# Mixing stage of a decoder trunk: transposes by 64 rows into two banks, v centred on quarters, weighted values by halves of the queries, v turned one tile later

## The chip, the cores and the metric

The kernel runs on one core of a Trainium2 chip. The core has a matrix engine (TensorE, PE in the profile), a vector engine (VectorE, DVE), an engine for activation functions and copies (ScalarE, ACT), a general one (GpSimd, POOL) and a queue engine for loads (SyncE, SP). They work side by side and wait for each other by semaphores; each runs its own instructions in order. TensorE reads from the on-chip memory SBUF and writes only to PSUM, eight banks of 128 partitions by 512 fp32 values; ScalarE or VectorE carry results from there back to SBUF.

The metric is the device time of one execution in microseconds (us), the median of several runs.

## What is computed

Two layers of a decoder trunk on 512 tokens of width 1024, in fp32. Each layer is a half-step SwiGLU feed-forward block, a token mixing, and a second feed-forward block. The change touches only the mixing, which has three groups of heads side by side:

```python
proj = hn @ w_mix_in[l]
p_att, p_rwkv, p_conv = jnp.split(proj, [...], axis=-1)
y_att = sliding_window_sink_attention(p_att, ...)   # 8 query heads, 2 key/value heads of 64, window 128
y_rwkv = rwkv7_time_mix(p_rwkv, ...)                # 4 heads of 64, a recurrence over time
y_conv = short_conv_mix(p_conv, conv_w[l])
h = h + (1.0 + gt2) * (jnp.concatenate([y_att, y_rwkv, y_conv], axis=-1) @ w_mix_out[l])
```

The attention works in blocks of 128 queries, each against its own block of keys and the one before:

```python
mask = (k_pos >= 0) & (diff >= 0) & (diff < WINDOW)          # diff = q_pos - k_pos, WINDOW = 128
scores = jnp.where(mask, scores, -jnp.inf)
probs = jax.nn.softmax(jnp.concatenate([scores, sink], axis=-1), axis=-1)[..., :-1]
out = jnp.einsum('bnhgqk,bnkhd->bnqhgd', probs, vb)
```

So query q of a block sees the keys 0 to q of its own block and the keys q+1 to 127 of the one before. The recurrence of the RWKV heads, with its per-step states, is computed in chunks of 64 tokens, as products of 64x64 matrices:

```python
S = S * w_t - s_kk * (kk_t * a_t) + v_t * k_t        # per head, outer products
y_t = S @ r_t
y = (y - mean(y)) * rsqrt(var(y) + eps)              # per head
```

The mean over a head is taken out early: v is multiplied by a centring matrix (constant `cen`, two 64x64 blocks on the diagonal).

## The kernel before

Activations lie with features on the partitions and the 512 tokens along the free dimension. The large products (weights times activations) split each fp32 operand in a high and a low part and take three fp32r products (lines 129 to 131 in the trace, `ps_mm`); the small products of the mixing are in plain fp32, and each of them stands in the trace as two MATMUL records. A transpose on TensorE is a product with the identity, one record each. All the small products go through the helper `pe`, line 806.

A mixing has a list of large products (the generator `products`: 20 projection tiles of eight steps with three products each, then the output projection) and three chains of small steps: `rwkv`, `attention`, and `inverse`. A planner at the end of `mix` weaves them. It keeps a clock: each large step of three products adds 0.65 us, each `yield cost, delay` of a chain adds `cost`, and the chain's next step is ready `delay` us later (times 1.1 for `rwkv`). When a step is ready it is issued, otherwise the next large products. A bare `yield` in `products` moves the clock without issuing anything. This order is what the compiler gets; its scheduler may still move an instruction whose inputs it believes late behind later ones, and `ORDER` dependencies pin some. PSUM has four pairs of banks by tag: `mm`, `r0`, `r1` and `x`; the RWKV chain uses `r0` and `r1`, the attention `x`.

The steps that the change touches:

- `turn_` (a helper): four whole 128x128 transposes of a [128, 512] tile into one bank.
- In `rwkv`, line 1171 on: `be` and the first half of `AR` of both head pairs q are turned with `turn_` (banks `ps_beN` and `ps_ta`), then copied by ScalarE to `beN` and `AX`. Step costs: 1.8, 3.4.
- In `rwkv`, line 1202 on: `v` is centred and turned at once by a product with `cen` (`ps_vN`), `ka` is turned (`ps_kaN`), and ScalarE copies both, 512 columns at a time. Step costs: 2.6, 3.2. The next step, `ps_xv`, uses `vN`.
- In `products`, line 878 on: the attention's v is copied out of its projection tile to `vr`; after three bare yields it is turned into `V` (`ps_vt`). Then come the four query tiles, with the roots of the keys (`rk`) behind the first.
- In `attention`: for each block b, `scores` and `softmax` of both key/value groups g, then for g = 0 and g = 1 in turn the shares (line 1384) and `turned`: four whole transposes of the shares (`ps_pt`, one bank), and a product on VectorE with each causal mask (`mc` for the own block, `mp` for the one before, line 1369), 512 columns each. At the end the weighted values: for each mask and group a product of V (128 keys by 64) with 512 columns (4 heads x 128 queries) into one bank `ps_av`, and one copy by ScalarE to `qr` (line 1396). The products with V are held behind the last mask by an `ORDER` dependency (`together`). The next block's scores wait for that copy.

Of the kernel before, what the change touches and what calls it, by code (L numbers as in the profile page):

```python
# [12 lines left out]
ALU = mybir.AluOpType  # L13
# [4 lines left out]
P = 128  # L18
# [52 lines left out]
def trunk_kernel(ctx, tc, ins, out, layers=L, phases=("ffn1", "mix", "ffn2")):  # L71
# [677 lines left out]
    def mix(l, hn, ss, mp, then, ready):  # L749
# [65 lines left out]

        def roots(srcs, name, bias, scale, low=None):
# [26 lines left out]
        def products():  # L843
# [36 lines left out]
            yield  # L880
            yield
            yield
            large()
            pv = psum([P, NB, P], "ps_vt")
            turn_(pv, vr)
            V = blocks(A("V"))
            nc.scalar.copy(V, pv)
# [4 lines left out]
            for i in range(4):  # L892
# [4 lines left out]
                if i == 0:  # L897
                    large()
                    rk = roots([ksq], "rk", vals["eps"], 1.0 / CH)
# [136 lines left out]
        def rwkv():  # L1036
# [136 lines left out]
            pv, pt = banks("ps_beN"), banks("ps_ta")  # L1173
            for q in qs:
                turn_(blocks(pv[q]), be[q])
                turn_(blocks(pt[q]), AR[q][:, 0].rearrange("p c t -> p (c t)"))
            for q in qs:
                nc.scalar.copy(beN[q], blocks(pv[q]))
                for e in range(2):
                    nc.scalar.copy(AX[q][:, e, :, 0], blocks(pt[q])[:, :, rows[e]])  # L1180
            yield 1.8, 3.4
# [21 lines left out]
            pv, pt = banks("ps_vN"), banks("ps_kaN")  # L1203
            for q in qs:
                for b in range(NB):
                    pe(blocks(pv[q])[:, b], v_[q][:, b * P : (b + 1) * P], cst("cen"), start=True, stop=True)
                turn_(blocks(pt[q]), ka[q])
            for q in qs:
                nc.scalar.copy(vN[q], blocks(pv[q]))
                nc.scalar.copy(kaN[q], blocks(pt[q]))  # L1210
            yield 2.6, 3.2
# [100 lines left out]
        def attention():  # L1312
# [49 lines left out]
            def turned(b, Sc):  # L1362
                pt = psum([P, 4, P], "ps_pt")
                for i in range(4):
                    pe(pt[:, i], Sc[:, i], cst("ident"), start=True, stop=True, is_transpose=True)
                both = []
                for name, src in (("mc", b), ("mp", b - 1))[: 1 + (b > 0)]:
                    t = E("p" + name)
                    made[0] = tt(t.rearrange("p (i q) -> p i q", q=P), pt, rep(name, 4), ALU.mult)
                    if b == 2:  # L1370
                        held.append(made[0])
# [375 lines left out]
```

## Time and profile before

| | us |
|---|---|
| median of 3 runs | 1781.1 |
| lowest, highest | 1780.77, 1784.97 |
| the profiled execution, its own time | 1782.9 |
| its span, first to last instruction | 1781.1 |
| mixing, layer 0 (first to last small product) | 372 to 540 |
| mixing, layer 1 | 1250 to 1418 |

The profile's page has the busy time of each engine, and the trace behind it answers queries: groups of instructions by line or tile, waits, a timeline, windows. A timeline row gives the start, the time from the first start to the last end of a run of like instructions, engine, line, operation, output<-inputs, the part of the array used (128\*128 is the whole, 64\*128 half the rows, 64\*64 a quarter, 128\*64 half the columns), the shape streamed, and the count; in brackets the idle time ahead of it and what ended it. Products on TensorE are pipelined: a row's duration contains a latency that the next product overlaps, so costs are read from start to start. PEld are the weight loads.

### The profile page before, as it was taken

The numbers are of one execution on the slowest core, as the hardware profiler recorded it, in microseconds if no ns is written. First come the engines' busy times: TensorE is split into PE (matmuls) and PEld (weight loads), VectorE is DVE, ScalarE is ACT, GpSimd is POOL, SyncE is SP. The second block draws the span as 40 slices with busy tenths as digits, with TensorE's granted clock in tenths as the row PEclk, the third lists the DMA queues.
The fourth block names the chain that finished last, engine by engine and source line by source line (L and its number), as shares of the span: only waits on it lengthen the run. The fifth ranks groups of instructions, "written<-read, shape, count | busy, mean of one in ns | idle before, by whom it ended". The sixth has DMA issues, their size and how long they took to land.

```text
span 1781.1 us, 35078 instructions
## 1 busy us (share of the span) xinstructions
PE 1756.9 (99%) x14480; PEld 1599.6 (90%) x14480; DVE 1384.2 (78%) x2224; ACT 856.1 (48%) x1324; POOL 148.6 (8%) x233
## 2 busy tenths in 40 slices
PE   9999999999999999999999999999999999999998
PEld 7898999987778999899899989999777789999998
DVE  7877687877769887677888777887686788865897
ACT  7452355364444554255355515544644345533653
POOL 0101001100000011110100010010000000000000
PEclk9999999999999999999999999999999999999999
DMA  9767867532133676877737597773421427675664
GB/s 379 221 183 266 230 191 213 182 94 85 43 120 112 179 188 220 258 203 204 240 119 200 166 304 194 205 227 106 122 69 29 143 83 217 187 231 139 196 175 111
DMA packets 95440, 313.14 MB, mean 176 GB/s; under 512 B 10864, under 2 KB 13168, under 8 KB 94256
## 3 DMA queue, kind: packets, MB, share of 16 engines
q1 hardware_dynamic: 65088, 203.68, 33.8%
q0 software_dynamic: 30192, 107.23, 24.2%
q8 instruction: 113, 1.85, 0.4%
q14 instruction: 47, 0.39, 0.1%
HBM read 306.93 MB, written 3.93 MB: 175 GB/s over the span
## 4 chain that ended last, share of the span: by engine, by line
PE 83%; DVE 9%; ACT 3%; issue 2%; DMA 2%; POOL 0%; SPq 0%; DVEq 0%; ACTq 0%; POOLq 0%
PE ps_mm L129 13%; PE ps_mm L130 13%; PE ps_mm L131 13%; PE ps_d L436 7%; PE ps_d L438 7%; PE ps_d L437 7%; PE ps_f L438 3%; PE ps_f L436 3%; PE ps_f L437 3%; PE ps_mm L1562 2%; DVE wL L143 2%; PE ps_g L436 2%; PE ps_g L438 2%; PE ps_g L437 2%; ACT wH L141 1%
## 5 line engine op out<-in xcount | busy, mean ns | idle before, releaser
L141 ACT CAST wH<-wraw 128x1024 fp32r<-128x1024 f32 (+2 forms) x273 | 251.8, 927 | 441.1 <-PE ps_mm L130 200.2
L143 DVE TENSOR_TENSOR wL<-wraw,wH 128x1024 fp32r<-128x1024 f32 (+2 forms) x273 | 291.4, 1071 | 111.1 <-ACT wH L141 110.1
L129 PE MATMUL ps_mm<-actH,wH 128*128 128x512 f32 (+1 forms) x700 | 253.8, 363 | 1.3 <-DVE h L345 1.2
L130 PE MATMUL ps_mm<-actL,wH 128*128 128x512 f32 (+1 forms) x700 | 252.9, 361 | 0.9 <-DVE actL L442 0.9
L131 PE MATMUL ps_mm<-actH,wL 128*128 128x512 f32 (+1 forms) x700 | 252.8, 361 | 0.0
L129 PE MATMUL ps_mm<-hnH,wH 128*128 128x512 f32 (+1 forms) x712 | 247.4, 353 | 1.1 <-ACT hnH L293 0.8
L130 PE MATMUL ps_mm<-hnL,wH 128*128 128x512 f32 (+1 forms) x712 | 245.5, 347 | 0.3
L131 PE MATMUL ps_mm<-hnH,wL 128*128 128x512 f32 (+1 forms) x712 | 244.7, 346 | 0.6 <-DVE wL L143 0.6
L436 PE MATMUL ps_d<-comH,wH 128*128 128x256 f32 x864 | 238.5, 276 | 0.0
L437 PE MATMUL ps_d<-comL,wH 128*128 128x256 f32 x864 | 237.6, 275 | 0.0
L438 PE MATMUL ps_d<-comH,wL 128*128 128x256 f32 x864 | 237.6, 275 | 0.0
L143 DVE TENSOR_TENSOR wL<-sum,wH 128x1024 fp32r<-128x1024 f32 x110 | 134.5, 1224 | 81.2 <-ACT wH L141 81.0
L141 ACT CAST wH<-sum 128x1024 fp32r<-128x1024 f32 x110 | 115.1, 1047 | 121.3 <-PE ps_f L437 39.3
L200 DVE SCALAR_TENSOR_TENSOR wada<-wada,crep 128x1024 f32<-128x1024 f32 x128 | 153.0, 1218 | 21.7 <-DMA wada<-in_wadaT 21.1
L436 PEld LDWEIGHTS ps_d<-comH,wH 128*128 128x128 f32 x864 | 165.8, 192 | 1.7 <-ACT s L462 1.6
L438 PEld LDWEIGHTS ps_d<-comH,wL 128*128 128x128 f32 x864 | 165.9, 192 | 0.0
L437 PEld LDWEIGHTS ps_d<-comL,wH 128*128 128x128 f32 x864 | 165.9, 192 | 0.0
L129 PEld LDWEIGHTS ps_mm<-hnH,wH 128*128 128x128 f32 x712 | 133.0, 190 | 21.9 <-issue 7.6
L129 PEld LDWEIGHTS ps_mm<-actH,wH 128*128 128x128 f32 x700 | 132.6, 189 | 17.8 <-DVE h L345 2.1
L131 PEld LDWEIGHTS ps_mm<-hnH,wL 128*128 128x128 f32 x712 | 135.2, 190 | 14.1 <-DVE wL L143 1.0
L130 PEld LDWEIGHTS ps_mm<-actL,wH 128*128 128x128 f32 x700 | 132.7, 190 | 16.5 <-DVE actL L442 1.2
L130 PEld LDWEIGHTS ps_mm<-hnL,wH 128*128 128x128 f32 x712 | 135.2, 190 | 13.5 <-DVE hnL L294 1.4
(428 smaller groups left out, 3981.6 us busy)
## 6 DMA issues: line engine op xcount, KB each, us to landing
wada<-in_wadaT POOLq DMA_DIRECT2D x126, 512.0 KB, 4.7
wraw<-in_wmi SPq DMA_DIRECT2D x40, 512.0 KB, 3.6
wraw<-in_w2p SPq DMA_DIRECT2D x36, 512.0 KB, 3.7
wraw<-in_w1p SPq DMA_DIRECT2D x32, 512.0 KB, 4.4
wraw<-in_w1o SPq DMA_DIRECT2D x32, 384.0 KB, 5.0
wraw<-in_w2o SPq DMA_DIRECT2D x32, 384.0 KB, 4.1
wraw<-in_w1o SPq DMA_DIRECT2D x32, 320.0 KB, 3.8
sum<-in_w2p SPq DMA_DIRECT2D x18, 512.0 KB, 4.4
```

The costliest lines, as they stand in the source:

```text
L129: mm(acc, wH, xH, start=start, stop=False)
L130: mm(acc, wH, xL, start=False, stop=False)
L131: latest["large"] = mm(acc, wL, xH, start=False, stop=stop)
L141: latest["cast"] = nc.scalar.copy(hi, src)
L143: return nc.vector.tensor_sub(lo, src, hi.bitcast(F32))
L200: stt(w, w, 1.0, crep, ALU.mult, ALU.mult, accum_out=out_)
L436: mm(acc, wH, xH, start=start and i + k == 0, stop=False, skip_group_check=True)
L437: mm(acc, wH, xL, start=False, stop=False, skip_group_check=True)
L438: mm(acc, wL, xH, start=False, stop=k == 3, skip_group_check=True)
L1562: latest["large"] = pin("PE", mm(paired(pts[n]), w, x, start=first, stop=last, skip_group_check=True))
```

## The change

Four edits, all in `mix`. The numbers of operations on VectorE stay; the step costs and delays given to the planner are adapted.

1. `turn_heads` turns by 64 rows: for each block of 128 tokens and each half of the features (e = 0, 1) a transpose of its own, with 64 rows of the array and 64 columns of the identity, into a bank per half. It is used for `be` and `AR` (instead of 16 whole transposes, 32 by 64 rows) and for `ka`. `join` copies the two banks to the old places: two copies of 256 columns instead of one of 512.
2. `by_heads` with both halves of the tokens as parts centres v on four 64x64 quarters of the array.
3. In the attention, both groups' shares are made in one step; `turned` then turns both groups together, with 16 transposes of 64 query rows in place of 8 whole ones: those of the first half of the queries go into one bank, those of the second half into the other. The masks are applied by halves of the queries, to both groups at a time. `values` has one bank for each half n of the queries: the second half meets all keys of its own block, the first half all keys of the block before, and the first half only the first 64 keys of its own block, the second half only the last 64 keys of the block before; what is left out is masked to zero. Two copies of 256 columns replace the one of 512.
4. The turn of the attention's v goes from behind three bare yields, after its own tile, to behind the first query tile; the bare yields are dropped.

```diff
@@ -813,6 +813,24 @@
             for b in range(NB):
                 pe(pt[:, b], x[:, b * P : (b + 1) * P], cst("ident"), start=True, stop=True, is_transpose=True)
 
+        heads = lambda pt: pt.rearrange("p (q b z) -> p q b z", q=2, z=CH)
+
+        def by_heads(pts, xs, rhs, parts=rows, **kw):
+
+            for b in range(NB):
+                for q in range(2):
+                    for c in parts:
+                        for e, r in enumerate(rows):
+                            pe(heads(pts[e])[c, q, b], xs[q][r, b * P : (b + 1) * P][:, c], rhs[r, r], start=True, stop=True, **kw)
+
+        def turn_heads(pts, xs):
+            by_heads(pts, xs, cst("ident"), (slice(0, P),), is_transpose=True)
+
+        def join(to, pts, q):
+
+            for e, r in enumerate(rows):
+                nc.scalar.copy(to[:, :, r], heads(pts[e])[:, q])
+
         def roots(srcs, name, bias, scale, low=None):
 
             n = len(srcs)
@@ -877,14 +895,6 @@
             pt = yield from tile_()
             vr = EA("vr")
             nc.scalar.copy(pt.like(vr), pt.view)
-            yield
-            yield
-            yield
-            large()
-            pv = psum([P, NB, P], "ps_vt")
-            turn_(pv, vr)
-            V = blocks(A("V"))
-            nc.scalar.copy(V, pv)
             qr = mp.tile([P, 4, T], F32, name="qr", tag="qr")
             rq = small("rq", NB * 8)
             rq4 = rq.rearrange("p (b i g) -> p b i g", i=4, g=2)
@@ -896,6 +906,10 @@
                     latest["act"] = copied
                 if i == 0:
                     large()
+                    pv = psum([P, NB, P], "ps_vt")
+                    turn_(pv, vr)
+                    V = blocks(A("V"))
+                    nc.scalar.copy(V, pv)
                     rk = roots([ksq], "rk", vals["eps"], 1.0 / CH)
                 if i == 1:
                     large()
@@ -1171,14 +1185,13 @@
             vN, beN, kaN = ([blocks(S(q, n)) for q in range(2)] for n in ("vN", "beN", "kaN"))
             qs = both()
             pv, pt = banks("ps_beN"), banks("ps_ta")
+            turn_heads(pv, be)
+            turn_heads(pt, [x[:, 0].rearrange("p c t -> p (c t)") for x in AR])
             for q in qs:
-                turn_(blocks(pv[q]), be[q])
-                turn_(blocks(pt[q]), AR[q][:, 0].rearrange("p c t -> p (c t)"))
-            for q in qs:
-                nc.scalar.copy(beN[q], blocks(pv[q]))
+                join(beN[q], pv, q)
                 for e in range(2):
-                    nc.scalar.copy(AX[q][:, e, :, 0], blocks(pt[q])[:, :, rows[e]])
-            yield 1.8, 3.4
+                    nc.scalar.copy(AX[q][:, e, :, 0], heads(pt[e])[:, q])
+            yield 1.0, 3.8
             while "r" not in done:
                 yield 0, STEP
             bo = [S(q, "bonus") for q in range(2)]
@@ -1201,14 +1214,12 @@
 
             qs = both()
             pv, pt = banks("ps_vN"), banks("ps_kaN")
+            by_heads(pv, v_, cst("cen"))
+            turn_heads(pt, ka)
             for q in qs:
-                for b in range(NB):
-                    pe(blocks(pv[q])[:, b], v_[q][:, b * P : (b + 1) * P], cst("cen"), start=True, stop=True)
-                turn_(blocks(pt[q]), ka[q])
-            for q in qs:
-                nc.scalar.copy(vN[q], blocks(pv[q]))
-                nc.scalar.copy(kaN[q], blocks(pt[q]))
-            yield 2.6, 3.2
+                join(vN[q], pv, q)
+                join(kaN[q], pt, q)
+            yield 1.5, 3.6
             qs = both()
             pts = quarters("ps_xv")
             for q in qs:
@@ -1359,42 +1370,59 @@
                 if other is not None:
                     tc.add_manual_dep(m.ins, other.ins.name, kind, reason="both groups run together")
 
-            def turned(b, Sc):
-                pt = psum([P, 4, P], "ps_pt")
+            def turned(b, both):
+                pts = [psum([P, 2, 4, CH], "ps_pt") for _ in range(2)]
                 for i in range(4):
-                    pe(pt[:, i], Sc[:, i], cst("ident"), start=True, stop=True, is_transpose=True)
-                both = []
-                for name, src in (("mc", b), ("mp", b - 1))[: 1 + (b > 0)]:
-                    t = E("p" + name)
-                    made[0] = tt(t.rearrange("p (i q) -> p i q", q=P), pt, rep(name, 4), ALU.mult)
-                    if b == 2:
-                        held.append(made[0])
-                    both.append((t, src))
-                return both
+                    for g, Sc in enumerate(both):
+                        for r, pt in zip(rows, pts):
+                            pe(pt[:, g, i], Sc[r, i], cst("ident")[r, r], start=True, stop=True, is_transpose=True)
+                shares = {}
+                for name, n in (("mc", 1), ("mp", 0), ("mc", 0), ("mp", 1)):
+                    if name == "mc" or b:
+                        t = E("p" + name).rearrange("p (g i q) -> p g i q", g=2, i=4)
+                        mask = cst(name)[:, rows[n]].unsqueeze(1).unsqueeze(1).to_broadcast([P, 2, 4, CH])
+                        made[0] = tt(t, pts[n], mask, ALU.mult)
+                        if b == 2:
+                            held.append(made[0])
+                        shares[name, n] = t
+                return shares
+
+            def values(b, shares):
+                po = [psum([P, 4, CH], "ps_av") for _ in range(2)]
+                begun = set()
+
+                def add(name, n, keys, last):
+                    src = b if name == "mc" else b - 1
+                    for g in range(2):
+                        t = shares[name, n][keys, g]
+                        m = pe(po[n][rows[g]], V[keys, src, rows[g]], t, start=n not in begun, stop=last)
+                        together(m, made[0])
+                    begun.add(n)
+
+                add("mc", 1, slice(0, P), not b)
+                if b:
+                    add("mp", 0, slice(0, P), False)
+                add("mc", 0, rows[0], True)
+                if b:
+                    add("mp", 1, rows[1], True)
+                for n in range(2):
+                    free[0] = nc.scalar.copy(qr[:, :, b * P + n * CH : b * P + (n + 1) * CH], po[n])
 
             for b in range(NB):
-                qs = slice(b * P, (b + 1) * P)
-                pm = []
                 both = yield from scores(b)
                 dens = [softmax(b, g, Sc) for g, Sc in enumerate(both)]
+                yield 1.06, 6.4
                 for g, (Sc, (den, es)) in enumerate(zip(both, dens)):
-                    yield 1.06 * (g == 0), 6.4 if g == 0 else 1.2
                     tt(den, den, es, ALU.add)
                     nc.vector.reciprocal(den, den)
                     share = tt(Sc, Sc, den.unsqueeze(2).to_broadcast([P, 4, P]), ALU.mult)
                     for later in turns if (b, g) == (2, 0) else ():
                         tc.add_manual_dep(later.ins, share.ins.name, ORDER, reason="shares go first")
-                    yield 0, 1.4
-                    pm.append(turned(b, Sc))
-                yield 0.4, 3.0
-                po = psum([P, 4, P], "ps_av")
-                for n in range(len(pm[0])):
-                    for g in range(2):
-                        t, src = pm[g][n]
-                        m = pe(po[rows[g]].rearrange("p i q -> p (i q)"), V[:, src, rows[g]], t, start=n == 0, stop=n == len(pm[0]) - 1)
-                        together(m, made[0])
-                free[0] = nc.scalar.copy(qr[:, :, qs], po)
-                yield 1.9, 1.0
+                yield 0, 2.6
+                shares = turned(b, both)
+                yield 0.5, 4.2
+                values(b, shares)
+                yield 1.4, 1.0
             done.add("ya")
 
 
```

## The prediction

> **What bounds the kernel now.** First the page's table of busy time, then the waits of TensorE in the mixing stretch of the first layer (engine and line, what it waited for, us in total, times, longest).
>
> ```profile
> PE 1756.9 (99%) x14480; PEld 1599.6 (90%) x14480; DVE 1384.2 (78%) x2224; ACT 856.1 (48%) x1324; POOL 148.6 (8%) x233
> PE ps_vt L806 <- ACT vr L879: 1.7, 1, 1.7
> PE ps_o L806 <- issue: 1.2, 1, 1.2
> PE ps_t L806 <- DVE X L1144: 1.1, 1, 1.1
> PE ps_av L806 <- DVE pmp L1369: 0.5, 1, 0.5
> PE ps_c L806 <- DVE K L1117: 0.5, 2, 0.3
> ```
>
> TensorE (PE) is busy 99% of the span, and its queue runs in order: what an edit takes off PE comes off the time, as long as no other engine is late there. In the mixing (372 to 552 us in layer 0, 1250 to 1430 in layer 1) PE stands still for some 5 us a layer in a handful of places, the longest at the turn of v. So I price every edit in PE time, counted from start to start, since one instruction's duration overlaps the next.
>
> **Prices on PE.** A step of whole transposes between large products:
>
> ```profile
> 404.52 0.38 PE L131 MATMUL ps_mm<-hnH,wL 128*128 128x512 f32 x1
> 404.74 0.60 PE L806 MATMUL ps_beN<-con,a 128*128 128x128 f32 x4
> 405.17 0.60 PE L806 MATMUL ps_ta<-con,AR 128*128 128x128 f32 x4
> 405.61 0.60 PE L806 MATMUL ps_beN<-con,a 128*128 128x128 f32 x4
> 406.04 0.60 PE L806 MATMUL ps_ta<-con,AR 128*128 128x128 f32 x4
> 406.40 0.46 PE L129 MATMUL ps_mm<-hnH,wH 128*128 128x512 f32 x1
> 406.70 0.38 PE L130 MATMUL ps_mm<-hnL,wH 128*128 128x512 f32 x1
> ```
>
> Groups of four start 0.435 us apart: 0.109 us for each whole transpose. From 404.52 to 406.70 are 2.18 us; two large products take 0.43 of it (their starts are 0.216 apart), so 16 transposes cost 1.75 and going in and out costs nothing. The same count for a step of 64 products on 64x64 quarters:
>
> ```profile
> 441.81 0.38 PE L131 MATMUL ps_mm<-hnH,wL 128*128 128x512 f32 x1
> 442.12 1.16 PE L806 MATMUL ps_x<-T,B 64*64 64x64 f32 x64
> 443.21 0.48 PE L129 MATMUL ps_mm<-hnH,wH 128*128 128x512 f32 x1
> 443.53 0.38 PE L130 MATMUL ps_mm<-hnL,wH 128*128 128x512 f32 x1
> ```
>
> 1.72 us less 0.43 is 1.29. Sixteen fours at (1.16 - 0.22)/16 = 0.058 us are 0.93 (0.22 being the tail of the last one, estimated), so **0.36 us are paid for leaving and re-entering the whole array**. A change between two split shapes I put at 0.155 us (estimated from the rows of the weighted values below: 460.24 comes 0.095 later than the 0.43 after the last pair, and a first small weight load adds some 0.05 to 0.06).
>
> No 64-row transpose stands in this trace. The nearest rows are the first scores, which work by 64 rows, and the weight loads (PEld) of whole transposes:
>
> ```profile
> 414.62 0.71 PE L806 MATMUL ps_sc<-kt,qr 64*128 64x128 f32 x4
> 416.10 0.72 PE L806 MATMUL ps_sc<-kt,qr 64*128 64x128 f32 x8
> 412.98 0.20 PEld L806 LDWEIGHTS ps_rq<-con,qsq 128*128 128x128 f32 x2 [0.72 <-ACT qsq L914]
> L806 PEld LDWEIGHTS ps_beN<-con,a x16: 139/140/143, 404.5 to 1283.9; 128*128 128x128 f32 x16
> ```
>
> Eight score products in two row halves take what four of one half take (0.72 against 0.71): halves with banks of their own run side by side. Two weight loads of a transpose span 0.20 us, one takes 0.14, so the second starts 0.06 after the first. The moving side of a whole transpose is 128 columns in 0.109; 64 columns are half, 0.055. I take **0.058 us for a pair of 64-row transposes**. The bounds: 0.109 for a pair (half the columns, full price, still in pairs) and 0.109 for each alone (0.218 a pair).
>
> [...]
>
> **The change part by part**, per layer, on PE.
>
> *beN and the turned AR*: 16 whole transposes (1.75) become 32 by 64 rows: 16 pairs at 0.058 plus 0.36 = 1.29. **-0.46.**
>
> *vN and kaN*, now:
>
> ```profile
> 451.94 1.05 PE L806 MATMUL ps_vN<-con,v 128*128 128x128 f32 x8
> 452.83 0.60 PE L806 MATMUL ps_kaN<-con,iP 128*128 128x128 f32 x4
> 453.27 1.06 PE L806 MATMUL ps_vN<-con,v 128*128 128x128 f32 x8
> 454.16 0.60 PE L806 MATMUL ps_kaN<-con,iP 128*128 128x128 f32 x4
> 454.60 0.60 PE L806 MATMUL ps_pt<-con,Sc 128*128 128x128 f32 x4
> ```
>
> 451.94 to 454.60 is 2.66. An fp32 product counts as two records, so centring on quarters is 4 blocks x 2 groups x 4 quarters x 2 = 64 records, which is exactly the 0.93 of the step at 442.12; kaN is 8 pairs, 0.46; one change of shape 0.155, in and out 0.36: 1.91. **-0.75.**
>
> *Shares turned*: per block 8 whole transposes (0.87, nothing around them) become 8 pairs, 0.46, plus 0.36 = 0.82. **-0.05 each, -0.2 for four blocks**: the change of shape eats nearly all.
>
> *Weighted values*, now, in a block with both key blocks:
>
> ```profile
> 458.37 1.08 PE L806 MATMUL ps_av<-pmc,V 128*64 128x512 f32 x4
> 459.28 1.03 PE L806 MATMUL ps_av<-pmp,V 128*64 128x512 f32 x4
> 460.24 1.16 PE L806 MATMUL ps_xv<-vN,K 64*64 64x64 f32 x64
> L806 PE MATMUL ps_av<-pmp,V 128*64 128x512 f32 x24 | 7.3, 592 | 0.0
> ```
>
> The two masks are four pairs of 512 columns; 458.37 to 460.24 is 1.87, of which 4 x 0.43 = 1.71 is streaming (the second pair of a 1.03 row starts 0.43 after the first, since one takes 0.59). After: two pairs of 256 columns on the nearer keys, two on the farther, and the two half-key products as two fours of 256: 6 x 0.2135 = 1.28, plus one more change of shape 0.155. **-0.27 in each of three blocks.** Block 0 has one mask: 0.854 becomes 0.427 + 0.427 (its halves can't be run as fours) plus 0.155: **+0.155**. Together -0.66.
>
> *v turned later*. The rows: first and last product of the next projection tile that ran before the turn, the turn, ScalarE's copies around it, and the group over both layers.
>
> ```profile
> 380.44 0.38 PE L129 MATMUL ps_mm<-hnH,wH 128*128 128x512 f32 x1
> 381.95 0.38 PE L130 MATMUL ps_mm<-hnL,wH 128*128 128x512 f32 x1
> 384.02 0.66 PE L806 MATMUL ps_vt<-con,vr 128*128 128x128 f32 x4 [1.70 <-ACT vr L879]
> 382.37 1.12 ACT L833 COPY wide<-rn 128x512 f32<-128x512 f32 x2
> 383.40 0.57 ACT L879 COPY vr<-ps_mm 128x512 f32<-128x512 f32 x1
> L806 PE MATMUL ps_vt<-con,vr 128*128 128x128 f32 x8 | 1.3, 286 | 3.4 <-ACT vr L879 3.4
> ```
>
> The next product was due at 382.17 and the turn starts at 384.02: 1.85 us lost, in either layer. After, the turn stands behind all of that next tile: eight steps of three products, 8 x 0.648 = 5.2 us from 380.44 on, so not before 385.6; vr is there at 383.97. The three bare yields go too; they issued nothing. What is late next there is kk's transposes, whose input (wide, 383.49) comes just ahead of vr's copy. **-1.85.**
>
> *Other engines.* VectorE's masks keep their number and size (four of 512 a block, two in block 0). ScalarE's copies of 512 become two of 256, 12 + 8 for 6 + 4:
>
> ```profile
> L1396 ACT COPY qr<-ps_av 128x512 f32<-128x512 f32 x8 | 4.7, 586 | 31.1 <-PE ps_av L806 31.1
> L1334 ACT COPY Sc<-ps_sc 128x256 f32<-128x256 f32 x24 | 7.8, 375 | 15.9 <-PE ps_sc L806 15.8
> ```
>
> 20 x 0.375 - 10 x 0.586 = +1.6 us a layer on an engine busy 48%; the planner's larger delays behind the two steps (3.8, 3.6) cover it, and uncovered it costs that 1.6 at most. No DMA is moved or added. PE gets 132 more products and as many weight loads a layer (16 + 48 + 8 + 32 + 28), which may move the stop marked "issue" at ps_o, 1.2 us, either way; I count nothing.
>
> *Sum*: -0.46 - 0.75 - 0.2 - 0.66 - 1.85 = -3.92 a layer, **-7.8 us** for two. The profiled execution took 1782.9 us, 1781.1 of it span; the median shown is 1781.1, so the difference is put on the median: **1773.3 us**, 0.44% faster. Neighbours move this: a step next to one of its own shape saves its 0.36, a lost neighbour costs 0.18. Adding up the planner's costs and delays I find turned b=2 behind ps_x and values b=3 between ps_o and ps_s (gain), and values b=1 cut off from ps_xv (loss): up to 1 us a layer better. The stops at ps_t and ps_av, 1.6 a layer, may go as well: -6.6 a layer, 1767.9, is the low end.
>
> **The rivals.**
>
> *Masks on the path.* Today a group's two masks run while the other group's shares are made. After, all four stand between the turns and the first value, since the values' two banks are those that the masks read.
>
> ```profile
> L1369 DVE TENSOR_TENSOR pmc<-ps_pt,con 128x512 f32<-128x512 f32 x16 | 10.9, 680 | 1.6 <-PE ps_pt L806 1.6
> 460.00:490.00 30.00, 28.36 (x470) 21.75 (x472) 24.83 (x58) 12.78 (x37) 0.00 (x0) 1.00 0.10 28
> ```
>
> VectorE is busy 24.8 of 30 us there. If two masks more (1.36) end up as a stop in blocks 1 and 2, that is 2.7 a layer: 1778.7. Against: the delay grows too, 4.2 + 0.5 for 2.7 of masks where it was 3.0 + 0.4 for 1.36, the same 2 us of room.
>
> *A pair at 0.109.* 56 pairs a layer (16 + 8 + 32) cost 0.051 more each, 2.9: the sum is -1.06 a layer, 1779.0. [...]
>
> *v's stop moves.* If PE stops for kk's input or the next tile's weights instead, 3.7 come back: 1777.0. Against: kk's input is ready before vr's copy starts.
>
> *Slower: the halves of a transpose don't pair.* If the 112 transposes by 64 rows run one after another at the 0.109 that a whole one takes, they cost 12.2 a layer where I have 3.25: +8.96 - 3.92 = +5.0 a layer, 1791.2. It decides from (3.92 + 3.25)/112 = 0.064 us for each; at 0.058 alone the sum would be -0.67 a layer, 1779.8. For it: no such row exists, and every transpose here uses the whole array. Against: the scores' halves pair.
>
> **How the numbers follow.** About 0.3% (5.3 us) is what a measurement of this kernel can tell from no change. Forecast 0.68, its own range 1768 to 1775.5; masks 0.11, pair at 0.109 0.09, v's stop 0.06, all three within 0.3%; unpaired 0.06, slower. So faster 0.68, same 0.26, slower 0.06. The range reaches from 1767.5 to 1780, over the three rivals in the middle, and leaves out the unpaired case.
>
> **What would show it.** In the timeline of the changed kernel: ps_vt without idle time ahead of it; 32 records of beN and AR in about 1.2 us, in twos that start together; ps_vN as 64 records in 0.93; the values' last products as fours; VectorE's masks finished before the first value. Wrong would be: 64-row transposes in single file, a stop before ps_av in several blocks, or a new stop at kk.

## The result, and the profile after

The changed kernel takes **1799.4 us** (median of 5 runs, 1797.7 to 1801.1), the one before 1782.0 (5 runs, 1780.8 to 1785.0): a ratio of 1.0095, 95% interval 1.0081 to 1.0110. It is slower by about 17 us where 7.8 were to be won, and 19 above the upper end of the range.

The page of the changed kernel, its first lines:

```profile
span 1799.4 us, 35650 instructions
...
PE 1763.2 (98%) x14744; PEld 1602.1 (89%) x14744; DVE 1383.9 (77%) x2224; ACT 858.2 (48%) x1344; POOL 148.5 (8%) x233
```

Span less PE's busy time is what PE stands still: 1799.4 - 1763.2 = 36.2 us, where it was 1781.1 - 1756.9 = 24.2. VectorE's busy time is the same to 0.3 us, so it has not more work, but it is waited for more. Yet PE's busy time has gone up by 6.3, though the edits take work off it.

First, did the edits cost what was said? The timeline of PE in the changed kernel (start, time, engine and line, operation, part of the array, shape, count):

```profile
404.97 0.38 PE L131 MATMUL ps_mm<-hnH,wL 128*128 128x512 f32 x1
405.28 0.71 PE L806 MATMUL ps_beN<-con,a 64*128 64x64 f32 x16
405.83 0.67 PE L806 MATMUL ps_ta<-con,AR 64*128 64x64 f32 x16
...
406.74 0.38 PE L130 MATMUL ps_mm<-hnL,wH 128*128 128x512 f32 x1
...
457.20 0.38 PE L131 MATMUL ps_mm<-hnH,wL 128*128 128x512 f32 x1
457.51 1.16 PE L806 MATMUL ps_vN<-con,v 64*64 64x64 f32 x64
458.61 0.71 PE L806 MATMUL ps_kaN<-con,iP 64*128 64x64 f32 x16
...
459.57 0.38 PE L130 MATMUL ps_mm<-hnL,wH 128*128 128x512 f32 x1
```

From 404.97 to 406.74 are 1.77 us, less two large products (0.43) 1.34, where 1.29 was forecast; from 457.20 to 459.57 the same count gives 1.94 for 1.91. Turned shares, counted so at 430.91, cost 0.84 (forecast 0.82), the weighted values at 461.39 cost 1.81 (1.28 + 0.155 + 0.36 = 1.80). The 64-row transposes do run in pairs: of the 32 of beN and AR the two of a pair start at most 0.01 us apart, and the pairs follow each other by 0.06 (the second by 0.11). At the place of the old stop PE runs through as well:

```profile
385.18 0.38 PE L131 MATMUL ps_mm<-hnH,wL 128*128 128x512 f32 x1
385.40 1.04 PE L806 MATMUL ps_kk<-con,wide 128*128 128x128 f32 x8
...
386.92 0.60 PE L806 MATMUL ps_vt<-con,vr 128*128 128x128 f32 x4
```

So the prices of the steps on PE were right, and the time went elsewhere. The waits of PE in the first layer's mixing, changed kernel (waited for; us in total, times, longest):

```profile
PE ps_av L806 <- DVE pmc L1384: 2.1, 1, 2.1
PE ps_mm L129 <- DVE r L799: 1.8, 1, 1.8
PE ps_sc L806 <- DVE elim L1030: 1.4, 1, 1.4
PE ps_mm L131 <- DVE wL L143: 1.4, 1, 1.4
PE ps_s L806 <- ACT y L1281: 1.1, 1, 1.1
PE ps_o L806 <- issue: 1.0, 1, 1.0
PE ps_q L806 <- ACT qsq L920: 0.8, 1, 0.8
```

The stop at ps_vt (1.7) is gone, and others have come in its place: at the attention's opening (ps_q, ps_sc), 15 us on (ps_mm behind r, at 429.45), at the third block's values (ps_av), and near the end (ps_s, ps_mm behind wL).

The second half of the loss is in a column that the prediction didn't price. Windows over the opening: from and to, length, busy time of PE, PEld, DVE, ACT, POOL, then the **granted clock**, the DMA share and GB/s. First the changed kernel, then the one before:

```profile
410.00:415.00 5.00, 2.90 (x15) 1.89 (x14) 1.91 (x10) 2.91 (x6) 0.00 (x0) 0.95 0.24 65
415.00:420.00 5.00, 5.00 (x19) 3.54 (x19) 2.71 (x12) 0.00 (x0) 0.00 (x0) 0.50 0.00 0
420.00:425.00 5.00, 5.00 (x22) 4.27 (x21) 3.96 (x18) 2.68 (x9) 0.00 (x0) 0.86 0.00 2
```

```profile
410.00:415.00 5.00, 4.68 (x27) 2.46 (x26) 4.18 (x17) 3.30 (x6) 0.00 (x0) 1.00 0.33 108
415.00:420.00 5.00, 5.00 (x29) 4.02 (x29) 4.50 (x24) 1.65 (x3) 0.00 (x0) 1.00 0.00 0
```

After a stretch in which PE worked 2.90 of 5 us, its clock is halved for (0.05 + 0.50 + 0.14) x 5 / 0.5 = 6.9 us. PE is "busy" all the while (5.00 of 5 us in both windows from 415 on), so no wait shows it. The large products do:

```profile
414.54 1.22 PE L806 MATMUL ps_sc<-kt,qr 64*128 64x128 f32 x4 [1.45 <-DVE elim L1030]
415.69 0.79 PE L130 MATMUL ps_mm<-hnL,wH 128*128 128x512 f32 x1
416.27 0.63 PE L131 MATMUL ps_mm<-hnH,wL 128*128 128x512 f32 x1
416.70 0.63 PE L129 MATMUL ps_mm<-hnH,wH 128*128 128x512 f32 x1
```

They start 0.43 us apart where 0.216 is usual. The clock records of the trace have four such stretches, of 6.83 and 3.41 us in either layer: at the opening and behind the third block's values. The kernel before has none there. The core's line of clocks sums it up, the changed kernel first:

```profile
core 0: 1799.4 us, clock 0.994
```

```profile
die 0 (median of its cores): 1781.1 us, clock 1.000
```

0.006 of 1799.4 is 10.8 us of clock gone (20.5 us at half speed make 10.2). The profiled executions differ by 1801.1 - 1782.9 = 18.2 us: **+12.0 of stops, +10.2 of halved clock, -4.1 of cheaper steps** (this term is the forecast's 2.07 a layer, without the turn, whose stop is in the first term) make 18.1.

### The profile page after: what moved, and what is told of

Read it like the earlier page. It is cut to its first block, busy times and chain, and to the rows that moved or that the text cites. A ratio compares the mean times of both kernels' runs of the same rounds, so it can differ in the third digit from the quotient of the medians.

```text
span 1799.4 us, 35650 instructions
## 1 busy us (share of the span) xinstructions
PE 1763.2 (98%) x14744; PEld 1602.1 (89%) x14744; DVE 1383.9 (77%) x2224; ACT 858.2 (48%) x1344; POOL 148.5 (8%) x233
## 3 DMA queue, kind: packets, MB, share of 16 engines
q0 software_dynamic: 30192, 107.23, 23.9%
## 4 chain that ended last, share of the span: by engine, by line
PE 80%; DVE 10%; ACT 4%; DMA 3%; issue 2%; POOL 0%; SPq 0%; ACTq 0%; DVEq 0%; POOLq 0%
PE ps_mm L129 13%; PE ps_mm L130 13%; PE ps_mm L131 13%; PE ps_d L436 7%; PE ps_d L437 7%; PE ps_d L438 7%; PE ps_f L438 3%; PE ps_f L437 3%; PE ps_f L436 3%; DVE wL L143 2%; PE ps_g L437 2%; PE ps_g L436 2%; PE ps_g L438 2%; PE ps_mm L1590 2%; ACT wH L141 2%
## 5 line engine op out<-in xcount | busy, mean ns | idle before, releaser
L129 PE MATMUL ps_mm<-hnH,wH 128*128 128x512 f32 (+1 forms) x712 | 251.5, 359 | 5.8 <-DVE r L799 3.5
L131 PEld LDWEIGHTS ps_mm<-actH,wL 128*128 128x128 f32 x700 | 132.7, 190 | 15.5
```

Of the source, the lines that this page charges most:

```text
L129: mm(acc, wH, xH, start=start, stop=False)
L131: latest["large"] = mm(acc, wL, xH, start=False, stop=stop)
```

## The experiments

All are timed against runs of the kernel before on the same chip (medians 1782.1 to 1783.0). "Still" is span less PE's busy time, "clock" the mean granted clock, both of the profiled execution, which need not lie at the median (no_v's took 1797.1 us, no_v_due's 1784.5).

| kernel | median us | ratio, 95% interval | still | clock |
|---|---|---|---|---|
| before | 1782.0 | | 24.2 | 1.000 |
| changed | 1799.4 | 1.0095 (1.0081 to 1.0110) | 36.2 | 0.994 |
| v_only | 1789.3 | 1.0040 (1.0025 to 1.0055) | 26.4 | 0.998 |
| no_v | 1793.3 | 1.0064 (1.0049 to 1.0080) | 34.2 | 0.996 |
| att_only | 1781.1 | 0.9994 (0.9985 to 1.0004) | 24.6 | 1.000 |
| rwkv_only | 1780.0 | 0.9990 (0.9981 to 0.9999) | 23.9 | 1.000 |
| no_v_old | **1779.0** | 0.9979 (0.9969 to 0.9989) | 24.8 | 0.999 |
| no_v_first | 1792.3 | 1.0053 (1.0038 to 1.0068) | 35.5 | 0.998 |
| after_old | 1785.0 | 1.0017 (1.0007 to 1.0028) | 27.2 | 0.998 |
| no_v_x1late | 1785.7 | 1.0017 (1.0007 to 1.0026) | 29.6 | 0.999 |
| after_x1late | 1794.2 | 1.0064 (1.0049 to 1.0079) | 31.8 | 0.997 |
| no_v_due | 1788.3 | 1.0029 (1.0020 to 1.0039) | 27.0 | 0.999 |
| yields_kept | 1799.2 | 1.0092 (1.0077 to 1.0107) | 34.3 | 0.994 |
| att_wait | 1797.7 | 1.0089 (1.0074 to 1.0104) | 38.1 | 0.997 |
| wait_old | 1798.5 | 1.0094 (1.0079 to 1.0109) | 42.5 | 0.996 |
| v_yields | 1785.3 | 1.0013 (1.0001 to 1.0025) | 23.2 | 0.997 |
| yields_old | 1782.7 | 1.0008 (0.9995 to 1.0021) | 22.7 | 0.996 |
| v_refill | 1782.2 | 0.9994 (0.9984 to 1.0003) | 21.5 | 1.000 |

### The parts of the change, one by one

**v_only** is the kernel before with v turned behind the next tile and no bare yields; **no_v** the change without that; **att_only** has only the attention's edits; **rwkv_only** only beN, AR, vN and kaN with their new step costs.

```diff
--- before
+++ v_only
-            yield
-            yield
-            yield
-            large()
-            pv = psum([P, NB, P], "ps_vt")
...
                 if i == 0:
                     large()
+                    pv = psum([P, NB, P], "ps_vt")
+                    turn_(pv, vr)
```

> The kernel before with the fourth edit alone: v is turned behind the first query tile and the three bare yields are gone. Theory 1 (order): the bare yields held the attention's opening back by three large steps on the planner's clock; without them the roots of the queries and the first scores reach VectorE's queue beside the elimination that still waits for its data from DRAM, TensorE stops there for about 3 us and then runs for some us at half clock. It expects 1.9 us a layer won at the turn and 6 to 8 lost at the opening: 1790 to 1796 us, with granted clock under 0.6 for some 5 us about 40 us after the mixing begins. Theory 2 (the attention's new halves are at fault): the stop at the turn goes and nothing comes in its place, 1778 us. Theory 3 (the split transposes are dear where they meet other steps): also 1778.

> The changed kernel without the fourth edit: v is turned at its old place with its three bare yields, everything else is changed. Theory 1: the attention's opening is as in the kernel before (TensorE does not stop at the first scores, full clock); what is left is 2 us a layer won by the prices, and some 3 to 5 lost at the third block and at the step of the outputs: 1782 to 1788 us. Theory 2: nearly all of the loss stays and the turn's stop comes back, 1800 to 1803. Theory 3: likewise about 1800.

> The kernel before with the attention's halves alone (both groups turned together, masks and values by halves of the queries). Theory 1: the opening is not touched, 1780 to 1786 us, with a stop before the values of the third block. Theory 2: most of the 17 us is here, above 1792. Theory 3: below 1785, as only the attention's few turns are split.

> The kernel before with the two steps of the recurrent heads alone (be, AR and ka turned by 64 rows, v centred on quarters, their new numbers for the planner). Theory A (the split steps cost what their rows say, 1.34 and 1.94 us for 1.75 and 2.66, and hurt only together with the attention's new order): 1.1 us a layer won, 1779 to 1781, no time at half clock. Theory B (the recurrent chain, issued 2 us earlier on the planner's clock, is at fault by itself): a cluster of stops in the third block and half clock there, 1786 to 1794.

The attention's edits alone give 1781.1, the RWKV side alone 1780.0, both without a stretch of half clock. Together (no_v) they are 1793.3, 11 us slower than before, with three such stretches. The late turn alone is 7 us slower. So there are two causes: something between the two halves of the edits, and the late turn. None of the three theories gave no_v's number (1782 to 1788, or about 1800); the second is out by att_only, and the second and third by v_only.

### Between the halves: one line of the planner's costs

**no_v_old** computes what no_v does, in the same instructions, but declares the two RWKV steps at the costs and delays of before; **no_v_first** puts only the first pair back; **after_old** is the changed kernel with both pairs old.

```diff
--- no_v
+++ no_v_old
-            yield 1.0, 3.8
+            yield 1.8, 3.4
...
-            yield 1.5, 3.6
+            yield 2.6, 3.2
```

> As the kernel without the fourth edit, but the two steps of the recurrent heads give the planner their old numbers (1.8, 3.4 and 2.6, 3.2); what they do is unchanged. Theory A (where the steps fall, not what they cost): the third block loses its cluster of stops, since the steps of the recurrent heads come about 2 us later against the attention, and the prices show: 1776 to 1781 us. Theory B (the copies by halves, or the split steps themselves, make ScalarE or VectorE late): as without the old numbers, 1791 to 1796.

> The change without the late turn, with the old planner's numbers at the step of beN and AR alone and the new ones at the step of vN and kaN. Both old gave 1779.0, both new 1793.3. If the first step's numbers move the third block's masks behind the inversion's product (the step stands before the attention opens): 1778 to 1781. If the second step's do (it stands just ahead of the third block): 1790 to 1794, with the 2 us stop at the weighted values near 484. If each does a part: between, 1783 to 1788.

> The changed kernel with the four planner's numbers of the kernel before at its two leaving and re-entering steps of the RWKV side. If the two causes add (numbers: -14.3 us as without the late turn; late turn: +7 as on the kernel before): 1785 to 1788, a dip at the opening near 414 and none, or one, in the third block. If they do not add, because the late turn moves the planner's clock once more for the third block: over 1792, with the stops at the third block's masks and values there again.

Four numbers that no engine sees are worth **14.3 us** (1793.3 to 1779.0), and 14.4 in the changed kernel (1799.4 to 1785.0). no_v_first turned out to be the same program as no_v, instruction by instruction on every engine (1792.3, so a repeat of it): **the second pair does it all**, the step of vN and kaN. Declared 1.1 cheaper, it puts the planner's clock earlier for what follows it, and in the third block two neighbours change places. PE, first no_v, then no_v_old:

```profile
474.46 1.15 PE L806 MATMUL ps_x<-T,B 64*64 64x64 f32 x60 [0.46 <-DVE TT L1175]
475.54 0.80 PE L806 MATMUL ps_pt<-con,Sc 64*128 64x64 f32 x16
...
483.81 1.12 PE L806 MATMUL ps_av<-pmc,V 128*64 128x256 f32 x4 [2.08 <-DVE pmc L1388]
```

```profile
471.99 0.65 PE L806 MATMUL ps_pt<-con,Sc 64*128 64x64 f32 x14 [0.34 <-DVE Sc L1422]
473.41 1.16 PE L806 MATMUL ps_x<-T,B 64*64 64x64 f32 x64
478.22 0.53 PE L806 MATMUL ps_t<-TT,X 64*64 64x64 f32 x18 [0.85 <-DVE X L1162]
480.04 0.68 PE L806 MATMUL ps_av<-pmc,V 128*64 128x256 f32 x4 [1.30 <-DVE pmc L1388]
```

In no_v the inversion's product ps_x goes ahead of the turned shares, in no_v_old behind them. VectorE then has, in no_v:

```profile
477.82 2.60 DVE L1162 TENSOR_TENSOR X<-ps_x,con 64x256 f32<-64x256 f32 x6
480.46 0.75 DVE L964 SCALAR_TENSOR_TENSOR conv_y<-conv_u,par,conv_y 128x511 f32<-128x511 f32 x1
481.12 0.68 DVE L1388 TENSOR_TENSOR pmc<-ps_pt,con 128x512 f32<-128x512 f32 x1
481.73 0.74 DVE L965 SCALAR_TENSOR_TENSOR conv_y<-conv_u,par,conv_y 128x510 f32<-128x510 f32 x1
...
483.58 0.68 DVE L1388 TENSOR_TENSOR pmp<-ps_pt,con 128x512 f32<-128x512 f32 x1
```

VectorE works without a gap, but one step of the convolution stands ahead of the masks and one among them, and the last mask ends at 484.26; in no_v_old the four masks follow X at once, 478.10 to 480.59. There PE also fits 18 products of the next step in front of the values. In no_v it stands still for 2.08 us, and from 483.2 on its clock is halved for 6.8 us by the clock records.

VectorE's order alone doesn't make this stop: the kernel before has the same one (two rows of VectorE, then PE):

```profile
481.07 0.75 DVE L946 SCALAR_TENSOR_TENSOR conv_y<-conv_u,par,conv_y 128x511 f32<-128x511 f32 x1
481.74 0.68 DVE L1369 TENSOR_TENSOR pmc<-ps_pt,con 128x512 f32<-128x512 f32 x1
...
483.73 1.24 PE L806 MATMUL ps_av<-pmc,V 128*64 128x512 f32 x3 [0.54 <-DVE pmp L1369]
```

Its values start at the same time as in no_v, but PE has waited for 0.54 us only, since three large products stand there between the inversion's step and the values, and none in no_v. The stop comes of both engines' orders together.

Is it that exchange alone? **no_v_x1late** and **after_x1late** keep the new costs and make the inversion's second product due 1.6 later, which puts the shares ahead of it again (like any delay it moves later steps too); **no_v_due** keeps the new cost of 1.5 and makes the follower, xv, due after 4.4 instead of 3.6.

```diff
--- no_v
+++ no_v_x1late
-  yield (2.4 - 1.0 * lev if q == qs[0] else 0), 2.8 - 1.2 * lev
+  yield (2.4 - 1.0 * lev if q == qs[0] else 0), (2.8 - 1.2 * lev) + (1.6 if lev == 0 and q == qs[1] else 0)
```

```diff
--- no_v
+++ no_v_due
-            yield 1.5, 3.6
+            yield 1.5, 4.4
```

> The change without the late turn, all new numbers, and the inversion's second product x1 due 1.6 later, so that the third block's shares are turned and masked ahead of it and its values stand ahead of the inversion's next product; the step xv still stands ahead of the third block's first scores. If the masks behind x1 are the cause of the 14.3 us: 1778 to 1782, the 2.08 us stop at the third block's values down to about 1.3, no more than one half-clock stretch. If the earlier difference or something else carries it: 1788 to 1794.

> The change without the late turn, with the step of vN and kaN declared at its true cost of 1.5 and its follower due after 4.4 instead of 3.6, which puts xv behind the third block's first scores and the masks ahead of x1, as with the old numbers; on PE its order differs from that run only in the number of large products between some steps and in the order inside the step of t1.0 and values. If the order of steps is what matters and not the declared cost: 1778 to 1782. If the declared cost matters by the products it leaves between steps: 1785 to 1793.

> The changed kernel with all its numbers and x1 due 1.6 later. If the third block's order carries the 14.4 us that the old numbers win here, and the late turn its own 6: 1784 to 1788, the dip at the opening still there and the third block's gone. If not: 1795 to 1800.

Half of it: 1785.7 from 1793.3 without the late turn, and about a third, 1794.2 from 1799.4, with it, both outside either theory's numbers. The other way gives 1788.3, as was expected if the order of the steps is not all that matters. The stop at the values stays (1.7 us in no_v_x1late and 2.1 in no_v_due, third block), and a new one comes at the shares:

```profile
PE ps_av L806 <- DVE pmc L1388: 1.7, 1, 1.7
PE ps_pt L806 <- DVE Sc L1422: 1.4, 1, 1.4
```

(The waits of PE in no_v_x1late, third block.) Turning the shares earlier makes PE wait for the shares themselves. So the pair of steps is a third to a half of the cause; that the other differences of the block's order (xv ahead of the scores, the inversion's updates among the softmax on VectorE, the large products between the steps) carry the rest is argued and not shown: they were not taken further apart.

### The late turn

The first thought was that without the bare yields the attention starts too early on the planner's clock. **yields_kept** is the changed kernel with them back at their place; **att_wait** delays the attention's first step by 5 instead, **wait_old** does so with the old step costs.

```diff
--- changed
+++ yields_kept
             nc.scalar.copy(pt.like(vr), pt.view)
+            yield
+            yield
+            yield
```

```diff
--- changed
+++ att_wait
+            yield 0, 5.0
             for b in range(NB):
```

> The changed kernel with one thing put back: three bare yields stand where they stood, though v is still turned later. They issue nothing; they only move the planner's clock. Theory 1: the opening is again as before and the turn's stop is gone: 3 to 4 us under the kernel without the fourth edit, 1778 to 1785. Theories 2 and 3: as the changed kernel, 1797 to 1801.

> The changed kernel with one line more: the attention begins with a step that does nothing and asks for 5 us of delay, so that its first scores stand some eight large steps later in TensorE's queue, behind the landing of the elimination's data. Theory 1 (the opening comes too early): the stops at the first scores and the 6.8 us at half clock behind them go, and 4 to 6 us a layer come back: 1787 to 1792, less if the third block changes too. Rival (the loss at the opening is the elimination's lateness itself, wherever the scores stand): within 2 us of the changed kernel.

> The changed kernel with both: the attention's first step 5 us later, and the old numbers for the two steps of the recurrent heads. If the prices on TensorE were right and only the order lost them, no time at half clock is left and the time is 1771 to 1779 us; if the third block keeps its cluster of stops, 1783 to 1790.

The first thought fails in all three: 1799.2 and 1797.7 are what its rivals expected, and 1798.5 is outside both numbers of wait_old. In att_wait and wait_old the stop at the first scores comes some 8 us later and is longer (2.65 us in att_wait), and others follow, up to 42.5 us still. A delay moves the neighbours of all later steps as well, so it doesn't tell the opening apart. The next runs therefore leave the planner's clock untouched. **v_yields** is the kernel before with v turned late and the yields kept; **yields_old** the whole change with yields and old costs; **v_refill** is v_yields with v transposed five times over, 16 whole transposes too many, in place of the stop that went.

```diff
--- v_yields
+++ v_refill
-                    turn_(pv, vr)
+                    for _ in range(5):
+                        turn_(pv, vr)
```

> The kernel before with v turned later and the three bare turns of the large products kept where they stood, so that the planner's clock is that of before and only PE's own arrival at the attention's opening is earlier, by the 1.85 us of the stop that goes. Theory 'earlier arrival' (VectorE and the DMAs behind the elimination are late for any PE that comes 1.85 us sooner): 1785 to 1789.3 as with the turns dropped, a stop of over 1 us at the first scores near 412 and a half-clock stretch near 414. Rival 'the turns' (it is the planner's clock, moved by the three dropped turns, that puts the attention's first step among the products too early): 1778 to 1779, the 1.85 us a layer kept, no half-clock stretch.

> The changed kernel with the three bare turns kept and the old four numbers, v turned late: the planner's clock is that of the run without the late turn and with old numbers (1779.0 us). Theory 'earlier arrival': the opening's stop and dip are there as with the turns kept and new numbers (near 413.7), 1783 to 1788. Rival 'the planner's clock alone': 1775 to 1776, the 3.7 us of the stop at the turn of v won on top of 1779.0.

> As v turned late with the three bare turns kept (1785.3 us), but v is transposed five times over into the same bank, so that the 1.85 us of the stop that went are filled by 16 more whole transposes at 0.109 = 1.74 us of work: TensorE comes to the attention's opening as late as in the kernel before, and nothing is computed otherwise. Theory 'the early arrival starts the half clock': the work makes the kernel faster, 1782 to 1783.5, with a stop before the first scores of under 0.4 us a half and no half-clock stretch near 414 and 1295. Rival 'the opening's dip has to do with the place of the turn itself, or comes by chance': 1788 to 1789, the 3.5 us added, dips as before.

These tell the theories apart: it is PE's earlier arrival, and not the planner's clock. PE in v_yields stands still **less** than in the kernel before (1785.2 - 1762.0 = 23.2 us, where it was 24.2) and yet takes longer: its clock is 0.997, with 10.2 us of half clock in the mixing by the records, so 5.1 us gone (-1.0 and +5.1 are the 4.1 us between the two spans). The opening in v_yields, timeline of PE:

```profile
411.54 0.66 PE L806 MATMUL ps_rq<-con,qsq 128*128 128x128 f32 x4 [0.32 <-ACT qsq L913]
412.13 0.71 PE L806 MATMUL ps_sc<-kt,qr 64*128 64x128 f32 x4
412.77 0.48 PE L130 MATMUL ps_mm<-hnL,wH 128*128 128x512 f32 x1
414.15 0.75 PE L806 MATMUL ps_sc<-kt,qr 64*128 64x128 f32 x4 [0.90 <-DVE rq L919]
```

and what it waits for, on VectorE:

```profile
409.48 0.17 DVE L1015 TENSOR_TENSOR elim<-G,inv 128x15 f32<-128x15 f32 x1 [5.70 <-DMA G<-dl]
...
413.61 0.22 DVE L1016 TENSOR_TENSOR inv<-inv,elim 128x63 f32<-128x63 f32 x1
413.75 0.35 DVE L919 RECIPROCAL rq<-ps_rq 128x32 f32<-128x32 f32 x1
```

The roots' reciprocal has its input at 412.2 and runs at 413.75, in line behind the elimination, whose data comes by DMA through DRAM at 409.48. In the kernel before the elimination begins at 409.18 and the reciprocal runs at 413.68, with PE 1.4 us later at this place: the time at which VectorE is through is set by the DMA, not by PE. PE in v_yields comes earlier and waits for 0.90 us; it is busy 3.78 of the 5 us from 410 to 415, and from 415 to 420 its clock is 0.50. v_refill adds 3.5 us of useless work to v_yields and is **3.1 us faster** (1782.2 from 1785.3), its clock at 1.000 throughout:

```profile
412.97 0.66 PE L806 MATMUL ps_rq<-con,qsq 128*128 128x128 f32 x4 [0.32 <-ACT qsq L914]
413.56 0.71 PE L806 MATMUL ps_sc<-kt,qr 64*128 64x128 f32 x4
...
414.61 0.71 PE L806 MATMUL ps_sc<-kt,qr 64*128 64x128 f32 x4
```

yields_old has the old costs, the late turn and all cheaper steps: it stands still 22.7 us, least but for v_refill, and gives 1782.7 (just under the 1783 to 1788 expected of an early arrival), for its clock is 0.996 (two stretches of 6.83 in the second layer). Against no_v_old the late turn costs 3.7 us there, and 6.0 without the yields (after_old), of which 0.9 is the kernel before being slower among those runs (1782.95 for 1782.08). In the changed kernel itself the opening is worse by a DMA: the write of dl to DRAM, which POOL waits for before it can fetch G. POOL, changed kernel, then before:

```profile
408.25 1.16 POOL L1023 DMA_DIRECT2D G<-dl  x1 [5.50 <-DMA dl<-B]
```

```profile
405.48 1.16 POOL L1009 DMA_DIRECT2D G<-dl  x1 [3.18 <-DMA dl<-B]
```

The elimination starts at 412.91 instead of 409.18. In the first layer it starts as before when the yields are kept (409.07 in yields_kept), and late when they are gone (412.13 in v_only). But in the second layer the write is late with the yields kept as well: POOL waits for it 4.21 us in v_yields and 5.04 in yields_kept, where it is 2.65 in the kernel before and 2.59 in v_refill. The elimination then starts at 1289.86 in v_yields for 1287.18 before, and PE's stop at the scores is 2.18 us. So with v turned late the data itself can come later, and the filler puts that right too; what these writes meet on their way was not tried. The first layer's stop at the opening is shorter in yields_kept (0.86 us for 1.45), and the half clock comes all the same (0.50 from 415 to 420).

**A version that beats both**: no_v_old, 1779.0 us, 0.9979 (0.9969 to 0.9989) of the time before. It is the three cheaper parts with the old step costs and v turned where it was.

## Why the prediction was wrong

- **Prices on PE** (beN and AR -0.46, vN and kaN -0.75, shares -0.05, values -0.27 and +0.155): right to 0.05 us each. With the planner's numbers kept (no_v_old) they bring 3.1 us by the medians (1782.1 less 1779.0) and 3.7 by the profiled executions (1782.9 less 1779.2), one stretch of half clock (3.4 us, 1.7 lost) included, where 4.1 were forecast.
- **v turned later, -1.85**: the stop goes as said, kk isn't late, nothing stops in its place nearby. This step failed, in the sentence "What is late next there is kk's transposes": what is late next stands 26 us further on, VectorE's line behind the elimination's DMA. The gain of 3.7 becomes a loss of 2.4 us with the yields kept (v_yields against its runs of before, 1782.95) and of 7 without them (v_only).
- **"Neighbours move this"**, put at "up to 1 us a layer better": this is the step that failed by most. The new step costs were counted as harmless (larger delays that "cover" ScalarE's copies), and the neighbours were gone through by the shape of the array alone. The prediction even names the exchange, "turned b=2 behind ps_x", and books it as a gain: b=2 is the third block, and this is the order of no_v. What VectorE has to do between two neighbours wasn't gone through, though it is busy 24.8 of 30 us in the third block by a row of the prediction. The step costs are worth 14.3 us, of which undoing the exchange wins back 7.6.
- **The clock** isn't in the sum at all. The trace of before shows none of it in its mixing, but the price of a stop was taken as its length, and with 6.83 us of half clock behind it, it was up to 3.4 us more.
- **Rivals.** "Masks on the path" names the right place in the third block (ps_av behind pmc, 2.1 us) and its price of 2.7 a layer was the right kind; it was held for small since the delays looked equal, and it came by a change of order rather than by longer masks. The other blocks have no such stop. "A pair at 0.109" and "halves don't pair" are out by the rows above. "v's stop moves" was near the truth in kind, but looked only at the next step. Only the unpaired halves had a cost above the gain, so the slower side held 6% for a mechanism that did not occur.

A pair of 64-row transposes took 0.06 us: 16 pairs in the step of 1.34, of which the prediction's 0.36 is for going in and out. And the stops ahead of a stretch of half clock were short: the longest ahead of the first layer's stretch in v_yields is 0.90 us.

## What to carry to other kernels

Where a planner places steps by declared costs, a new cost is an edit of the order: list which steps change places, and look what the other engines do between them in that stretch, before any unit price. A stop taken off the critical engine is won only if the next thing that it meets is ready earlier too; here that was data that comes by a DMA, and it was not (the elimination began at 409.48 in v_yields and at 409.18 before). And read the granted clock beside the stops: in v_yields, where small steps with waits stand close together at the opening, PE was busier (1762.0 us for 1756.9), stood still less (23.2 for 24.2) and took longer (a span of 1785.2 for 1781.1), at a clock of 0.997.

## What the runs showed of the hardware

- In these runs PE's clock was halved for 3.41 or 6.83 us at a time, after a few us in which PE was partly idle: 2.90 of 5 us busy in the changed kernel at 410 us, 3.78 of 5 in v_yields, with no single stop over 1.5 and 0.9 us. At 4.68 of 5 (before) it wasn't. The stop of 1.70 at ps_vt between large products, in before and no_v_old, never halved it.
- PE's busy share alone didn't decide. In the changed kernel the clock records change at 414.53, 421.36, 489.63 and 493.04 us, and at 1302.00, 1308.82, 1377.09 and 1380.50: whole multiples of 3.413 us apart. The kernel before has one change, at 1781.28, behind its last instruction. In the step of 3.41 us from 381.81 to 385.22, counted back from it, with the stop at ps_vt, PE is busy 1.71 us, and the clock stays whole; it is halved behind 2.25 of 3.42 us in v_yields (from 411.27) and even behind 2.76 of 3.41 in no_v (from 1298.94, longest stop 0.65 us, and v at its old place; the clock is 0.73 from 1300 to 1305). What decides stays open.
- The same program has these stretches in different number: no_v's profile has 13.7 us of them, its repeat (no_v_first) 6.8. The runs of yields_old, with two long ones in its profile, spread over 1780.3 to 1789.4.
- A pair of 64-row fp32 transposes into two banks cost what one 64x64 four cost, about 0.06 us (16 pairs in the step of 1.34 us; 16 fours of ps_x in one of 1.29, in the kernel before).
